# Layer A of a hybrid decoder step: value and gate units cut into eighths between the chunks of the recurrence

## The chip, the cores and the metric

The kernel runs on one core of one Trainium2 chip. A core has five engines that run at the same time, each through a list of instructions of its own in order: TensorE (PE in the profile; matrix products, with PEld for the loading of its stationary operand), VectorE (DVE), ScalarE (ACT), GpSimd (POOL) and SyncE (SP), which mostly issues transfers (DMA) between the large memory (HBM) and the core's own memory. Products land in banks of a small accumulator memory (PSUM), from which ACT or DVE copies them out ("evacuation"). The metric is the device time of one execution in microseconds.

## The reference, cut to what matters

One step of a two-layer decoder trunk for a prompt of 512 tokens and 8 sample sequences of 4 tokens (544 columns in all), width 1024, 16 heads of 64. Layer A is a recurrent mixer, layer B an attention layer. The change is in layer A alone:

```python
mixed = xn[None] + mu[:, None, None, :] * (prev - xn)[None]     # token shift, six mixtures
rkvz = jnp.einsum('pbtd,pde->pbte', mixed[:4], w_in)            # r, k, v, gate z: four 1024 x 1024 products
...
def wkv_step(state, inp):                                       # one token, every head; state is 64 x 64
    r, w, k, v, kk, b = inp
    sa = jnp.einsum('bhij,bhj->bhi', state, kk)
    state = state * w[:, :, None, :] - sa[..., None] * b[:, :, None, :] + v[..., None] * k[:, :, None, :]
    return state, jnp.einsum('bhij,bhj->bhi', state, r)
...
y = ((y - y_mean) * lax.rsqrt(y_var + GN_EPS)).reshape(B, T, D) * gn_w + gn_b
y = y + (jnp.sum(rh * kh * r_k, axis=-1, keepdims=True) * vh).reshape(B, T, D)
out = (y.astype(x.dtype) * jax.nn.silu(z)) @ w_out
return x + out, xn[:, -1], wkv, v
```

## The kernel before, in words

All activations lie feature by token: eight tiles of 128 features by 544 tokens. Each of the four input products and the output product is cut into eight units of 128 output features: units 0 to 7 are k, 8 to 15 r, 16 to 23 v, 24 to 31 the gate z, 32 to 39 the output. A unit is one call of `dense` (line 143): weights and activations are both split into a high and a low part, and three products (high x high, high x low, low x high) are summed, for eight slices of the inner dimension and two halves of the tokens (256 and 288 columns): 48 matmuls, all on line 152. For the units in `BOTH` the two halves go side by side in two banks; for the others one half follows the other. There are two such banks (`NPD`). `load_w` (line 126) fetches a unit's 512 KB, casts the high part on ACT (line 133) and subtracts for the low part on POOL (line 134).

The prompt's recurrence is done in chunks of 64 tokens, for eight pairs of heads (numbered p), eight chunks each. For a pair, `pre_a`, `pre_b` (with `gram`) and `pre_e` prepare decays, scaled keys and products within the chunks; `tinv` inverts the triangular parts of a group of two pairs (four groups) by 31 steps on DVE; `tmerge` and `prechain` join them. `feed(p, i)` makes what two chunks need of the values and keys (lines 624 to 644). `step(p, c2)` runs two chunks after one another: line 656 (first product) to PSUM, ACT's copy to `uv` (line 659), line 661 (second product), DVE's update of the state `mv` (line 671), and lines 675 and 678 (the output). Line 656 of the next chunk of the same pair needs line 671 of this one. `bonus(p)` prepares the term with the values, `gn` and `gn_apply` the norm per head, `sample_lanes` and `gn_sample` the sample tokens, `gate(p)` multiplies with the gate. After that the output product runs (from line 863), and layer B.

The order of the work is written out by hand in `PLAN` (line 60), one letter and number for a call: K k-units, H the hidden layers of decay and a, r r-units, v v-units, z gate units, X0 the splitting of v's input (`xvsplit`), X2 the mixing of z's input to a scratch (`zmix`), X1 its splitting (`xzsplit`), X3 that of r, a/b/e the preparation, T, M, P inverse and merges, F feeds, C steps, o bonus, h and S the samples, G, I, Y norms, g gates. A scheduler then orders the instructions of each engine by this order, by what depends on what and by an own estimate of times; an instruction that is ready may be put ahead of one that comes earlier in the plan. The eight split tiles of x (`NX`) are shared by k, r, v and z in turn, so v's split waits for the last r unit and z's for the last v unit. Value tiles have three buffers (`NV`), and `bonus` and held gate units share two (`NZ`, tag "Z").

In this plan the v units stand among the feeds and steps of the first pairs, and the gate units at the end and among the last steps. A gate unit that comes before its group's norm is held in a buffer until `gate` (lines 799 to 809).

## Time and profile before

| | |
|---|---|
| median of 3 runs | 1506.39 us (1498.46 to 1509.73) |
| the profiled execution | 1502.82 us, span from first to last instruction 1501.0 us |
| mean granted TensorE clock | 0.925 |
| busy over the span | PE 1373.4 (91%), PEld 1161.3, DVE 989.5, ACT 654.1, POOL 531.5 us |
| layer A, layer B | to about 664 us, and from there to the end |
| first and last chunk matmul (line 656) | 258.7 and 570.3 us |

All times within the profile count from the span's start. A line of a table gives for each engine the time in which it was executing something and the number of instructions; for TensorE the ends are modelled, so a busy TensorE may still be a slow one: the clock that its throttle granted stands beside it, as a share of full speed. In a timeline, lines start with the start and the duration in us; "idle before" names what the engine waited for.

### The profile page before, as it was taken

The numbers are of one execution on the slowest core, as the hardware profiler recorded it, in microseconds if no ns is written. First come the engines' busy times: TensorE is split into PE (matmuls) and PEld (weight loads), VectorE is DVE, ScalarE is ACT, GpSimd is POOL, SyncE is SP. The second block draws the span as 40 slices with busy tenths as digits, with TensorE's granted clock in tenths as the row PEclk, the third lists the DMA queues.
The fourth block names the chain that finished last, engine by engine and source line by source line (L and its number), as shares of the span: only waits on it lengthen the run. The fifth ranks groups of instructions, "written<-read, shape, count | busy, mean of one in ns | idle before, by whom it ended". The sixth has DMA issues, their size and how long they took to land.

```text
span 1501.0 us, 32052 instructions
## 1 busy us (share of the span) xinstructions
PE 1373.4 (91%) x12144; PEld 1161.3 (77%) x12144; DVE 989.5 (66%) x2612; ACT 654.1 (44%) x1808; POOL 531.5 (35%) x763
## 2 busy tenths in 40 slices
PE   2999879998988998999889899999999999999986
PEld 2777868676767666989777779989799888998776
DVE  7428594747677546798996869756568554685434
ACT  5448353333342355444543435545355543644321
POOL 6124365434545221796867686000000000000121
PEclk9999978765879698999999999999999999999988
DMA  4123636224243113456344583445734356344632
GB/s 145 46 80 132 201 97 157 62 56 122 66 123 72 38 43 116 150 165 202 90 136 147 171 269 120 145 142 164 256 111 151 129 194 232 103 152 136 227 116 102
DMA packets 140587, 201.26 MB, mean 134 GB/s; under 512 B 76864, under 2 KB 80640, under 8 KB 140432
## 3 DMA queue, kind: packets, MB, share of 16 engines
q1 hardware_dynamic: 121456, 137.48, 29.9%
q10 hardware_dynamic: 16416, 54.41, 10.8%
q0 software_dynamic: 2560, 7.31, 1.4%
q8 instruction: 96, 1.57, 0.4%
q14 instruction: 59, 0.48, 0.1%
HBM read 150.90 MB, written 34.87 MB: 124 GB/s over the span
## 4 chain that ended last, share of the span: by engine, by line
PE 42%; DVE 8%; DMA 3%; ACT 1%; issue 1%; SPq 1%; ACTq 0%; DVEq 0%
PE dps L152 29%; DVE wlo L139 4%; PE sps L1014 3%; PE ptp L1075 2%; PE spo L1170 2%; PE ops L1091 1%; DMA swp<-nat 1%; PE ops L1087 1%; PE sc L1126 1%; SPq L945 1%; PE sc L1137 1%; PE sc L1132 1%; PE vtp L975 1%; DVE swp L947 1%; DMA vc<-in_vc 1%
## 5 line engine op out<-in xcount | busy, mean ns | idle before, releaser
L152 PE MATMUL dps<-hn,whi 128*128 128x256 f32 (+1 forms) x2560 | 509.3, 294 | 8.2 <-DVE vt L964 2.4
L152 PEld LDWEIGHTS dps<-hn,whi 128*128 128x128 f32 x2560 | 405.3, 189 | 31.0 <-issue 19.0
L152 PE MATMUL dps<-hn,wlo 128*128 128x288 f32 (+1 forms) x1280 | 373.6, 292 | 5.0 <-DVE wlo L139 4.6
L138 ACT ACTIVATE whi<-wst,prm 128x128 fp32r<-128x128 f32 x640 | 202.1, 391 | 223.2 <-PE dps L152 173.4
L139 DVE SCALAR_TENSOR_TENSOR wlo<-wst,prm,whi 128x128 fp32r<-128x128 f32 x640 | 252.7, 450 | 35.2 <-ACT whi L138 34.6
L152 PE MATMUL dps<-x,whi 128*128 128x256 f32 (+1 forms) x1024 | 229.7, 317 | 27.4 <-ACT x L166 11.0
L152 PEld LDWEIGHTS dps<-hn,wlo 128*128 128x128 f32 x1280 | 242.8, 190 | 12.7 <-DVE wlo L139 7.6
L152 PEld LDWEIGHTS dps<-x,whi 128*128 128x128 f32 x1024 | 178.1, 207 | 52.1 <-issue 15.9
L134 POOL TENSOR_TENSOR wlo<-wst,whi 128x1024 fp32r<-128x1024 f32 x48 | 118.5, 2469 | 191.9 <-ACT whi L133 179.3
L152 PE MATMUL dps<-x,wlo 128*128 128x288 f32 (+1 forms) x512 | 158.2, 310 | 0.0
L152 PEld LDWEIGHTS dps<-x,wlo 128*128 128x128 f32 x512 | 106.4, 208 | 2.6 <-issue 1.8
L1100 POOL COPY qd<-Q 64x32 f32<-64x32 f32 x48 | 12.7, 265 | 266.4 <-DVE Q L950 143.2
L1298 POOL TENSOR_TENSOR sS<-sS,sT 128x256 f32<-128x256 f32 x128 | 102.6, 802 | 8.3 <-DMA sS<-in_stN 0.2
L152 PE MATMUL dps<-g,whi 128*128 128x288 f32 (+1 forms) x512 | 102.2, 296 | 2.9 <-DVE ho L869 1.4
L133 ACT CAST whi<-wst 128x1024 fp32r<-128x1024 f32 x48 | 50.3, 1047 | 93.8 <-PE dps L152 61.3
L152 PEld LDWEIGHTS dps<-g,whi 128*128 128x128 f32 x512 | 82.1, 191 | 6.4 <-DVE g L167 2.9
L946 DVE TENSOR_TENSOR nat<-nat,cosn 128x544 f32<-128x544 f32 x48 | 36.5, 760 | 66.4 <-DMA swp<-nat 65.5
L152 PE MATMUL dps<-g,wlo 128*128 128x256 f32 (+1 forms) x256 | 74.1, 290 | 0.0
L1029 ACT ACTIVATE s<-s,nm 128x256 f32<-128x256 f32 (+1 forms) x128 | 61.7, 484 | 20.1 <-DVE nm L1026 20.0
L1107 POOL COPY pk<-vt 128x32 f32<-128x32 f32 x24 | 5.4, 225 | 161.1 <-DVE vt L964 108.6
L1014 PE MATMUL sps<-K,Q 64*128 64x128 f32 (+1 forms) x384 | 55.1, 321 | 6.4 <-DVE st L1020 4.0
L307 DVE SCALAR_TENSOR_TENSOR mix<-xn,prm,mix 128x512 f32<-128x512 f32 x48 | 42.4, 884 | 26.0 <-ACT mix L305 25.9
(315 smaller groups left out, 2433.6 us busy)
## 6 DMA issues: line engine op xcount, KB each, us to landing
wst<-in_wb SPq DMA_DIRECT2D x88, 512.0 KB
kc<-in_kc ACTq DMA_DIRECT2D x48, 512.0 KB
vc<-in_vc ACTq DMA_DIRECT2D x48, 512.0 KB
wst<-in_wa SPq DMA_DIRECT2D x40, 512.0 KB
swp<-nat SPq DMA_DIRECT2D x192, 68.0 KB
out_kT<-K SPq DMA_DIRECT2D x24, 272.0 KB
out_vT<-vt SPq DMA_DIRECT2D x24, 272.0 KB
xt<-in_xT SPq DMA_DIRECT2D x8, 272.0 KB
```

What stands on the lines that cost most here:

```text
L133: nc.scalar.copy(hi, st)
L134: nc.gpsimd.tensor_tensor(lo, st, hi.bitcast(F32), op=ALU.subtract)
L138: nc.scalar.mul(hi[:, kt], st[:, kt], g)
L139: nc.vector.scalar_tensor_tensor(lo[:, kt], st[:, kt], g, hi[:, kt].bitcast(F32), op0=ALU.mult, op1=ALU.subtract)
L152: nc.tensor.matmul(ps[:, :n], lhsT=a[:, kt, :], rhs=x[:, c0:c0 + n], start=(kt == 0 and i == 0), stop=(kt == KT - 1 and i == 2))
L307: nc.vector.scalar_tensor_tensor(m[:, 0:NP_], xn[kt][:, 0:NP_], pv(s, kt), m[:, 0:NP_], op0=ALU.mult, op1=ALU.add)
L946: nc.vector.tensor_tensor(nat, nat, cosn, op=ALU.mult)
L1014: nc.tensor.matmul(ps[h][:, j, o], lhsT=Q[g][r, q], rhs=K[g][r, ks], start=True, stop=True)
L1029: nc.scalar.activation(s[:, b, lo:], s[:, b, lo:], AF.Exp, bias=nm[:, b:b + 1], accum_out=stats[:, b, h, 1:2])
L1075: nc.tensor.transpose(ps[:, b], st["s", l, h][:, b, half * P:(half + 1) * P], self.ident)
L1170: nc.tensor.matmul(po[32 * j:32 * j + 32, 0:256], lhsT=pT[:, i, 32 * j:32 * j + 32], rhs=vc[:, j], start=(i == 0), stop=False, skip_group_ ...
L1298: nc.gpsimd.tensor_tensor(s, s, t, op=ALU.add)
```

## The change

The dense units of v 2 to 7 and of z 0 to 7 are no longer calls of the plan. `dense` becomes a generator, `dense_pieces`, that yields ahead of each eighth of a unit (six matmuls). With `pin`, the first matmul of an eighth is tied behind the instruction that was written just before it on TensorE, so that the scheduler can't put it earlier. The plan's new call Q puts the 14 units (and between them the splitting of z's input) into a queue. `step` calls `pump` behind line 656 and behind the second product of each chunk: each call adds 0.875 to what is due, and eighths are written until that many are out, so 128 calls for 112 eighths. The call D writes what is left. The weights of a unit are loaded when the last eighth of the unit before is written.

A finished v unit and a held gate unit go to scratches in HBM (`scr["v"]`, `scr["z"]`); `values(p)` loads the values back at the first feed of a pair, `gate` loads its gate unit. Value tiles have four buffers. The plan is written anew: pairs 0 and 1 prepared and v 0 and 1 done first; then group by group, the steps of a group's two pairs taking turns, with the preparation of the next group's pairs between them; then the norms and gates of all.

```diff
-NV = 3
+NV = 4
+RATE = 0.875
-PLAN = """H0 K0 K1 H1 H2 H3 H4 H5 K2 H6 H7 K3 K4 K5 K6 K7 X3 r0 r7 N a0 r1 a1 b0 e0 b1 e1 T0
-X2 r2 r3 a3 r4 a2 r6 r5 X0 v1 v3 v0 b3 e3 M0 P0 F0 F1 F2 v2 C0 C1 b2 o1 F3 C2 C3 M1
...
-h0 h4 h5 h2 h6 h7 h1 S M6 P6 F24 F31 C30 z5 F25 C24 z0 Y0 G1 F26 I1 z2 z1 C19 C25 F27 G2 I2
-z3 C26 G0 C27 C31 G3 z4 g4 I0 g5 g3 g0 g1 g2 z6 I3 z7 g7 g6
+PLAN = """H0 K0 K1 H1 H2 H3 H4 H5 K2 H6 H7 K3 K4 K5 K6 K7 X3 r0 r1 N r2 a0 a1 r3 b0 b1 T0 r4 r5 e0 e1 r6 r7
+X0 X2 v0 v1 Q M0 P0 M1 P1
+F0 F1 a2 F4 F5 C0 F2 a3 C4 F6 b2 C1 F3 C5 b3 F7 T1 C2 C6 e2 C3 e3 o0 C7 o1
+M2 P2 M3 P3 F8 F9 a4 F12 F13 C8 F10 C12 F14 b4 C9 F11 a5 C13 F15 b5 T2 C10 C14 e4 C11 e5 o2 C15 o3
+M4 P4 M5 P5 F16 F17 a6 F20 F21 C16 F18 C20 F22 b6 C17 F19 a7 C21 F23 b7 T3 C18 C22 e6 C19 e7 o4 C23 o5
+M6 P6 M7 P7 F24 F25 o6 F28 F29 o7 G0 C24 F26 h0 h1 h2 h3 h4 h5 h6 h7 C28 F30 S I0 C25 F27 C29 F31 G1 C26 C30 I1
+C27 C31 D Y0 G2 I2 G3 I3 g0 g1 g2 g3 g4 g5 g6 g7
     def dense(self, w, xs, evac, both=False):
+        for _ in self.dense_pieces(w, xs, evac, both):
+            pass
+
+    def dense_pieces(self, w, xs, evac, both=False, pin=False):
...
+                m = nc.tensor.matmul(ps[:, :n], lhsT=a[:, kt, :], rhs=x[:, c0:c0 + n], start=(kt == 0 and i == 0),
+                                     stop=(kt == KT - 1 and i == 2))
+                if pin and i == 0:
+                    self.tc.keep_in_program_order(m)
         for hfs in (((0, 1),) if both else ((0,), (1,))):
-            ps = {hf: self.pd.tile([P, 512], F32, name="dps", tag="d") for hf in hfs}
+            ps = {}
             for kt in range(KT):
+                first = both or kt % 2 == 0
+                if first:
+                    yield
                 for hf in hfs:
-                    mm(ps[hf], hf, kt)
+                    if kt == 0:
+                        ps[hf] = self.pd.tile([P, 512], F32, name="dps", tag="d")
+                    mm(ps[hf], hf, kt, pin and first and hf == hfs[0])
...
+            queue, sent, due = [], [0], [0.0]
+
+            def advance():
+                while queue:
+                    if callable(queue[0]):
+                        queue.pop(0)()
+                        continue
+                    if next(queue[0], None) is not None:
+                        sent[0] += 1
+                        return
+                    queue.pop(0)
+
+            def pump():
+                due[0] += RATE
+                while queue and sent[0] < due[0]:
+                    advance()
...
             def feed(p, i):
                 bk, rh = BK[p], RH[p]
+                values(p)
...
                         nc.tensor.matmul(ps[r, o:o + 64], lhsT=WW[p][:, e, c2, h, :], rhs=mv[:, e, h, :],
                                          start=(e == 0), stop=True, skip_group_check=True)
+                    pump()
                     for h, r in ((0, RA), (1, RB)):
                         self.mv_("ue", uv[RA, e, h, :], ps[r, o:o + 64], h)
...
+                    pump()
                     if c < 7:
...
                 if hold:
-                    Z[p] = zp.tile([P, NT], F32, name="zg", tag="Z")
+                    Z[p] = True
+                    zt = zp.tile([P, NT], F32, name="zg", tag="Z")
...
-                self.dense(self.load_w(W[24 + p]), xz, evac, both=24 + p in BOTH)
+                for _ in self.dense_pieces(lambda: self.load_w(W[24 + p]), xz, evac, 24 + p in BOTH, True):
+                    yield True
+                if hold:
+                    nc.sync.dma_start(out=scr["z"][p], in_=zt)
...
+            def vlater(p):
+                t = vp.tile([P, NT], F32, name="vT", tag="V")
...
+                for _ in self.dense_pieces(lambda: self.load_w(W[16 + p]), xv, evac, 16 + p in BOTH, True):
+                    yield True
+                nc.sync.dma_start(out=scr["v"][p], in_=t)
+
+            def values(p):
+                if vT[p] is None:
+                    vT[p] = vp.tile([P, NT], F32, name="vT", tag="V")
+                    nc.sync.dma_start(out=vT[p], in_=scr["v"][p])
...
+                       Q=lambda p: queue.extend([vlater(i) for i in range(2, 8)] + [xzsplit]
+                                                + [zproj(i) for i in range(8)]))
```

## The prediction, made before the changed kernel was run

> **What bounds the kernel now.** I read the profile's page first (slices), then the busy time of the engines by stage, then the dense matmuls alone, then the timeline and the waits of TensorE.

> ```profile
> PEclk9999978765879698999999999999999999999988
> ```

> From the sixth to the sixteenth slice (37.5 us each, so about 190 to 600 us) TensorE's granted clock is mostly below full. The stretches of the kernel, cut at the first chunk matmul (258.70), at the end of the last chunk (574), at the first output projection (607.7) and at layer B (664), with their columns length, PE, PEld, DVE, ACT, POOL, clock, DMA share, GB/s:

> ```profile
> 125.00:200.00 75.00, 66.61 (x500) 58.38 (x499) 53.44 (x109) 39.22 (x84) 33.20 (x33) 0.95 0.55 171
> 200.00:232.00 32.00, 25.29 (x148) 20.42 (x149) 31.45 (x74) 16.68 (x35) 18.93 (x20) 0.57 0.28 84
> 232.00:258.70 26.70, 24.25 (x322) 21.80 (x321) 8.09 (x22) 8.79 (x19) 17.61 (x19) 0.94 0.70 166
> 258.70:574.00 315.30, 286.11 (x3478) 214.19 (x3480) 198.66 (x599) 123.43 (x344) 125.46 (x214) 0.77 0.28 76
> 574.00:607.70 33.70, 30.75 (x203) 26.47 (x200) 23.20 (x38) 17.26 (x27) 9.02 (x7) 0.91 0.38 117
> 607.70:664.00 56.30, 52.15 (x390) 49.25 (x389) 45.87 (x57) 22.79 (x43) 48.98 (x47) 1.00 0.51 167
> 664.00:1501.00 837.00, 793.75 (x6575) 700.24 (x6574) 564.72 (x1600) 360.77 (x1139) 232.77 (x357) 0.98 0.49 159
> ```

> The recurrence takes 315.30 us at a mean clock of 0.77. TensorE is idle for only 29 us of it; its 286 us of work are 286.11 x 0.77 = 220 us at full clock. So 66 us go to the low clock and 29 to idling. The next views say when the clock is low. First the dense matmuls alone (tile dps; PE, clock, DMA share, GB/s) in 10 us steps:

> ```profile
> 300.00:310.00 10.00, 0.00 (x0) 0.50 0.29 68
> 310.00:320.00 10.00, 0.02 (x1) 0.50 0.14 40
> 320.00:330.00 10.00, 8.58 (x48) 0.80 0.28 69
> 330.00:340.00 10.00, 0.00 (x0) 1.00 0.42 91
> ```

> The clock is half while only small matmuls run, and returns when a whole dense unit (48 matmuls) comes by. Then, from the timeline, what half clock costs, in pairs of cold and warm rows:

> ```profile
> 301.64 0.48 PE L675 MATMUL cps<-rT,mv 64*64 64x64 f32 x4
> 302.05 0.48 PE L678 MATMUL cps<-Q,uv 128*64 128x64 f32 x4
> ...
> 542.69 0.33 PE L675 MATMUL cps<-rT,mv 64*64 64x64 f32 x4
> 542.95 0.34 PE L678 MATMUL cps<-Q,uv 128*64 128x64 f32 x4
> ```

> ```profile
> 320.79 0.63 PE L152 MATMUL dps<-x,whi 128*128 128x256 f32 x2
> ...
> 321.43 0.63 PE L152 MATMUL dps<-x,whi 128*128 128x256 f32 x2
> ```

> ```profile
> 577.89 0.51 PE L152 MATMUL dps<-x,whi 128*128 128x256 f32 x2
> ...
> 584.09 1.03 PE L779 MATMUL ssg<-sqg,sel 128*2 128x512 f32 x4
> ```

> A chunk's group of four starts 0.41 us after the one before when cold, 0.26 when warm; three dense matmuls take 0.64 us cold. A whole unit takes 584.09 - 577.89 = 6.2 us warm, so 0.78 us for an eighth. Of waits, TensorE has few in the recurrence:

> ```profile
> PE cps L675 <- DVE mv L671: 8.4, 8, 2.3
> PE atp L524 <- DVE ak L517: 4.7, 1, 4.7
> ```

> So the bound of this stage is TensorE at a low clock; the chain of a chunk comes second.

> **The change, part by part.** Everything before 125 us and after 664 us stays. I go by stages.

> (1) Up to the first chunk. Now it starts at 258.70. The new order has only pairs 0 and 1 prepared and units v0, v1 done by then; one unit (v3, 6.2 us) and the preparation of pairs 2 and 3 go behind the start, merges of pair 1 come ahead of it. The mix of the gate input (X2) comes later, behind X0, on ACT and VectorE, but only the eighths of z need it. In 200:232 VectorE is busy 31.45 of 32 us while TensorE has 25.29 us at clock 0.57; this is where the preparation of pairs 2 and 3 stands in the way of the split of x for v. With it gone I take 20 us off: 6 of v3 and 14 of the 32. At worst only the 6 go, at best 32 (all of that stretch's length). Start at 239 (227 to 253).

> (2) Work in the recurrence. Dense matmuls now:

> ```profile
> 258.70:574.00 315.30, 66.37 (x384) 59.39 (x384) 2.62 (x6) 6.42 (x18) 0.77 0.28 76
> ```

> 384 are 8 units. The queue holds 14 (six v, eight z), 112 eighths for 128 pumps at 0.875, so all go between chunks: 6 x 6.2 = 37 us more. Of the pairs' own work, two pre_a, gram and pre_e come in and two merges' share, the last group norm and the sample norm go out:

> ```profile
> L411 PE MATMUL lps<-hid,lb 64*128 64x288 f32 (+1 forms) x36 | 17.3, 624 | 1.8 <-ACT tw L413 1.8
> ...
> L607 PE MATMUL wwp<-TT,ak 64*64 64x64 f32 x512 | 16.2, 248 | 0.1
> ```

> Eight of L411's make a pre_a (3.8 us), L607 costs 2.0 us a pair; with their neighbours I take +13 and -10, net 3 (bounds -10 and 13). Work at full clock: 220 + 37 + 3 = 260 us.

> (3) What comes on top of it. Now it is 66 for the clock and 29 for idling, 95 on 220. An eighth stands behind the first and behind the second matmuls of a chunk (1.75 of them per chunk, 64 chunks), so while ACT copies and VectorE updates the state TensorE streams 0.78 us of dense work. In 315 us that is an eighth each 2.8 us; the stretches of 20 us without any dense matmul go. I take the clock's loss as 28 (66 less more than half). Idling: each pin holds what is queued behind it on TensorE: the next chunk's small matmuls, and who waits for them, ACT's copy of uv and VectorE's state update. A pinned eighth waits for its weights (cast on ACT, subtraction on POOL), for a free bank of two, that is for the last evacuation, and, at the ninth unit, for xz. I take 32 for idling (29 now), as the fill takes about as much as the new holds give. 260 + 28 + 32 = 320. Bounds: 260 + 10 + 15 = 285 and, if the loss stays at the present ratio, 260 x 315 / 220 = 372. So C31 ends at 239 + 320 = 559, where it is 574 now.

> (4) Other engines and queues in it. VectorE has 198.66 us now; pre_a and pre_b of two pairs and the evacuations of five gate units bring it to some 225 of 320, no bound. POOL subtracts the weights' parts of six more units there,

> ```profile
> L134 POOL TENSOR_TENSOR wlo<-wst,whi 128x1024 fp32r<-128x1024 f32 x48 | 118.5, 2469 | 191.9 <-ACT whi L133 179.3
> ```

> 6 x 2.47 = 15 us more on 125. What waits in POOL's line behind one of them for 2.5 us is the copy of a chunk's values (uv), and so L661; that is part of the 32 for idling. SyncE gets 28 DMA issues more (6 + 8 stores, 6 + 8 loads of 272 KB each). The DMA share is 0.28 here, and their issue is as bsum's now:

> ```profile
> L687 SPq DMA_DIRECT2D bsum<-scr_b x8: 319/382/526, 183.4 to 423.5; - x8
> L689 POOL TENSOR_TENSOR bsum<-bsum,vT x8: 1327/1336/2468, 233.2 to 451.1; 128x544 f32<-128x544 f32 x8
> ```

> 28 x 0.38 = 11 us on a queue of 320 us: hidden by loads that are issued early (the first bsum 50 us before its use). If the cover goes, an issue stands behind a wait of SyncE, whose largest sum is

> ```profile
> SPq L129 <- POOL wlo L134: 37.1, 4, 22.5
> ```

> and a feed waits for vT. I cost it at 0, at most one such 22.5.

> (5) From the last chunk to the output projection, now 33.7 us of which TensorE works 30.75, nearly all gate units. These are gone; what is left is the chain of the last norm:

> ```profile
> 575.15 2.71 PE L772 MATMUL cps<-Y,cblk 128*128 128x512 f32 x4
> ...
> 584.09 1.03 PE L779 MATMUL ssg<-sqg,sel 128*2 128x512 f32 x4
> ```

> ```profile
> 587.43 0.95 SPq L783 DMA_DIRECT2D rows<-rs  x2
> ```

> L779 needs L772's squares, ready at about 578.6, and stood 5.5 us behind a dense unit. So 33.7 - 5.5 = 28; reloads of z (two buffers) may add 6, so 28 to 36; I take 29. The projection then starts after some 20 us of idle TensorE, so one or two us cold: 58 for its 56.3.

> Sum: 239 + 320 + 29 + 58 = 646 for layer A where it is 664, so 18 us less, and the profiled execution (1502.82, span 1501.0) would take 1485. It lies 3.57 below the median of 1506.39, so I say 1488.

> [...] The clock falls here in a stretch that isn't idle (PE, clock, DMA share, GB/s in 2 us steps):

> ```profile
> 394.00:396.00 2.00, 1.70 (x26) 1.00 0.93 333
> 396.00:398.00 2.00, 1.30 (x20) 1.00 0.04 15
> 398.00:400.00 2.00, 1.33 (x21) 0.77 0.03 8
> ```

> TensorE was busy for two thirds of the time and lost the clock. [...]

> **The rivals.** (a) The clock holds throughout: loss 0 to 5, idling 32. The recurrence is 260 + 3 + 32 = 295, the whole 25 less than above: 1463. For it: at 330:340 the clock stays at 1.00 with no dense matmul at all, so little is needed to hold it. Against: the rows at 394.
> (b) No gain: the pins hold as much as the clock gives. The recurrence at 335 to 340, the whole 1503 to 1508. For it: the chains of the inverse stay on VectorE inside the groups, and L675 already waits for VectorE (8.4 us), atp too (4.7 at once).
> (c) Slower: once cold it stays cold. In the old order whole units brought the clock back (8.58 us of dense in 320:330); in the new one no dense run is longer than 0.78 us warm, so a window is a mixture. If the clock is half for three quarters of the recurrence, work goes at 0.26/0.41 = 0.63 of the pace there, 260 / (0.25 + 0.75 x 0.63) = 360, with 30 of idling 390: 70 more than above, 1558. It decides from 340 on, that is a loss of 80 on 260; at half the recurrence cold it is 260 / 0.815 + 30 = 349, 1517. A second way to the same place: z and bonus share two buffers (tag Z), and reloads issued far ahead, as bsum's, can keep both from the evacuation of a unit, which keeps a bank, which keeps a pin.

> **How the numbers follow.** Anything within 15 us (1%) of 1506 can't be told from no change. Forecast as summed (1470 to 1491) 0.35, (a) with all below 1470 0.17, (b) (1491 to 1521) 0.26, (c) above 1521 0.22. So faster 0.52, same 0.26, slower 0.22. The likeliest case's own range is 1470 to 1491. The range for 8 in 10 leaves out the far end of (a), below 1450 (0.08), and of (c), above 1535 (0.12).

> **What would show it.** Clock in the recurrence above 0.9 and its length near 320 (step 3); first L656 near 239 (step 1); 14 units' matmuls between first and last chunk (step 2); L779 right behind L772 at the end, no dense unit between (step 5). Wrong would be: a clock of 0.7 or below with eighths spread evenly (c); long rows of dense matmuls waiting for an evacuation, weights or xz, with L656 and L661 queued behind (b); a recurrence that starts no earlier than 255.

## The result, and the profile after

The changed kernel takes 1574.07 us (median of 4 runs, 1571.99 to 1576.79) and the kernel before 1507.7 in the same series (1498.46 to 1509.73). The ratio is 1.0454, with a 95% interval of 1.0406 to 1.0502: slower by 4.5%, where 1488 us had been forecast. The profiled execution has a span of 1575.0 us, 74.0 more than before.

The slices of the changed kernel's page, 39.4 us each (tenths busy, tenths of full clock):

```profile
PE   2999869989879798368988999999999999999986
...
PEclk9998966978669779669999999999999999999988
```

The low clock from the sixth to the sixteenth slice, which was to go, is still there, and two slices follow (630 to 710 us) with TensorE at 3 and 6 tenths. The stages, cut as the prediction cut them (length, PE, PEld, DVE, ACT, POOL, clock, DMA share, GB/s):

```profile
120.00:200.00 80.00, 70.91 (x522) 62.57 (x522) 59.44 (x118) 37.61 (x77) 33.23 (x34) 0.90 0.45 138
200.00:252.20 52.20, 39.47 (x485) 32.31 (x484) 40.47 (x71) 30.12 (x65) 28.95 (x39) 0.60 0.48 135
252.20:628.50 376.30, 334.11 (x3643) 256.93 (x3641) 214.74 (x620) 125.27 (x345) 138.91 (x224) 0.80 0.32 88
628.50:690.00 61.50, 22.88 (x75) 13.14 (x76) 28.29 (x46) 17.42 (x34) 20.09 (x24) 0.61 0.34 103
690.00:738.20 48.20, 44.15 (x336) 43.34 (x336) 32.98 (x44) 17.80 (x36) 44.48 (x45) 0.97 0.51 169
738.20:1575.00 836.80, 796.87 (x6576) 701.57 (x6574) 558.81 (x1600) 360.49 (x1139) 217.07 (x336) 0.98 0.48 158
```

The recurrence takes 376.3 us where it took 315.3. TensorE's clock is 0.80 after 0.77, so it hardly rose. From the last chunk to layer B it is 109.7 us where it was 90.0. The start is 6.5 us earlier, and layer B is as it was.

For comparing runs the recurrence is measured below from the start of the first chunk's first product (line 656 before, 693 after) to that of the last chunk's (some 4 us less than above), and "the end" from there to layer B's first matmul. These are the rows of before and after, all instructions and then the dense matmuls alone. First, before:

```profile
258.70:570.40 311.70, 282.82 (x3450) 212.27 (x3452) 196.74 (x592) 120.28 (x337) 125.46 (x214) 0.77 0.28 74
```

```profile
258.70:570.40 311.70, 66.37 (x384) 59.39 (x384) 0.77 0.28 74
```

Then after:

```profile
252.20:624.40 372.20, 330.91 (x3618) 254.50 (x3616) 213.25 (x615) 124.43 (x341) 138.91 (x224) 0.79 0.32 87
```

```profile
252.20:624.40 372.20, 132.46 (x660) 105.27 (x660) 0.79 0.32 87
```

The 60.5 us come apart from these rows. The dense matmuls take 132.46 us instead of 66.37 (+66.1), all other matmuls 330.91 - 132.46 = 198.5 instead of 216.4 (-18.0), and TensorE idles for 41.3 instead of 28.9 (+12.4). A dense matmul in the recurrence takes 132.46 / 660 = 201 ns, where it took 173. That the small matmuls got faster isn't shown: by the counts of the rows they are 108 fewer (2958 for 3066), and a dense matmul is counted here to its modelled end, which overlaps the small one behind it. Counted from each start to the next, a small one takes 70.8 ns where it took 71.5. Nor did the time at the low clock shrink: by the records of the granted clock, it is 154 us of these 372.2 (TensorE busy for 135 of them), and was 144 us (busy for 134).

With the start (-6.5), the recurrence (+60.5), the end (113.5 instead of 93.2, +20.3) and layer B (-0.3) this is the whole of the 74.0.

### The profile page after: what moved, and what is told of

Same layout as the page of the kernel before. It is cut to its first block, busy times and chain, and to the rows that moved or that the text cites. A ratio compares the mean times of both kernels' runs of the same rounds, so it can differ in the third digit from the quotient of the medians.

```text
span 1575.0 us, 32083 instructions
## 1 busy us (share of the span) xinstructions
PE 1399.3 (89%) x12144; PEld 1177.9 (75%) x12144; DVE 994.8 (63%) x2608; ACT 649.7 (41%) x1804; POOL 527.0 (33%) x763
## 4 chain that ended last, share of the span: by engine, by line
PE 40%; DVE 8%; DMA 2%; ACT 1%; issue 1%; SPq 0%; ACTq 0%; DVEq 0%
PE dps L158 28%; DVE wlo L140 3%; PE sps L1077 3%; PE ptp L1138 2%; PE spo L1233 2%; PE ops L1154 1%; PE ops L1150 1%; PE sc L1189 1%; DVE swp L1010 1%; DMA kc<-in_kc 1%; DMA swp<-nat 1%; DMA vc<-in_vc 1%; PE vtp L1038 1%; PE sc L1195 1%; PE sc L1200 1%
## 5 line engine op out<-in xcount | busy, mean ns | idle before, releaser
L158 PE MATMUL dps<-x,whi 128*128 128x256 f32 (+1 forms) x1024 | 248.7, 332 | 26.3 <-ACT x L179 15.1
L140 DVE SCALAR_TENSOR_TENSOR wlo<-wst,prm,whi 128x128 fp32r<-128x128 f32 x640 | 244.0, 437 | 34.6 <-ACT whi L139 34.2
L158 PE MATMUL dps<-g,whi 128*128 128x288 f32 (+1 forms) x512 | 107.3, 306 | 22.9 <-ACT g L179 14.6
L158 PEld LDWEIGHTS dps<-g,whi 128*128 128x128 f32 x512 | 85.8, 200 | 28.6 <-ACT g L179 16.9
L134 ACT CAST whi<-wst 128x1024 fp32r<-128x1024 f32 x48 | 50.2, 1045 | 86.2 <-PE dps L158 58.5
```

The costliest lines, as they stand in the source:

```text
L134: nc.scalar.copy(hi, st)
L140: nc.vector.scalar_tensor_tensor(lo[:, kt], st[:, kt], g, hi[:, kt].bitcast(F32), op0=ALU.mult, op1=ALU.subtract)
L158: m = nc.tensor.matmul(ps[:, :n], lhsT=a[:, kt, :], rhs=x[:, c0:c0 + n], start=(kt == 0 and i == 0), stop=(kt == KT - 1 and i == 2))
```

## The experiments

The table has for each run: the dense matmuls between first and last chunk, their time and ns of each; TensorE's other busy time and its idle time there; the mean granted clock; the recurrence; the end; the median. Except for the medians, the values are from window rows like those above. Times in us. Layer B, whose code no run changes, takes 834 to 850 us in these profiled executions, so a difference of some 15 us between two whole times need not be the edit's.

| run | dense | their time | ns each | other | idle | clock | recurrence | end | median |
|---|---|---|---|---|---|---|---|---|---|
| before | 384 | 66.4 | 173 | 216.4 | 28.9 | 0.77 | 311.7 | 93.2 | 1507.7 |
| after | 660 | 132.5 | 201 | 198.5 | 41.3 | 0.79 | 372.2 | 113.5 | 1574.1 |
| e1_nopin | 569 | 94.2 | 165 | 211.2 | 26.3 | 0.79 | 331.7 | 123.3 | 1555.4 |
| e2_whole | 571 | 94.5 | 165 | 217.0 | 30.3 | 0.77 | 341.8 | 121.9 | 1564.9 |
| e3_oldorder | 624 | 127.1 | 204 | 210.3 | 19.3 | 0.77 | 356.6 | 92.7 | 1546.8 |
| e5_early | 660 | 131.0 | 199 | 198.9 | 48.7 | 0.79 | 378.6 | 118.4 | 1596.3 |
| e8_oldhalf | 378 | 84.0 | 222 | 223.3 | 24.2 | 0.72 | 331.5 | 101.9 | 1529.9 |
| e9_oldhalf_nopin | 416 | 70.0 | 168 | 216.3 | 35.5 | 0.76 | 321.8 | 92.7 | 1527.6 |
| e10_rate | 423 | 87.7 | 207 | 212.9 | 51.4 | 0.75 | 351.9 | 131.9 | 1579.3 |
| e6_tail | 648 | 129.2 | 199 | 206.8 | 43.4 | 0.79 | 379.4 | 91.9 | 1566.3 |
| e4_apart | 0 | 0 | | 266.8 | 58.6 | 0.57 | 325.3 | 167.6 | 1626.8 |
| e11_burst | 660 | 130.9 | 198 | 196.9 | 46.3 | 0.79 | 374.1 | 117.3 | 1579.7 |
| e12_wholepin | 618 | 107.6 | 174 | 205.3 | 51.4 | 0.78 | 364.2 | 117.1 | 1572.4 |
| e13_nopin_tail | 545 | 90.0 | 165 | 222.8 | 31.7 | 0.78 | 344.4 | 95.3 | 1543.2 |
| e14_cover | 283 | 49.7 | 176 | 261.2 | 49.9 | 0.65 | 360.8 | 103.0 | 1558.7 |
| e15_ctrl | 478 | 80.5 | 168 | 219.8 | 26.2 | 0.77 | 326.5 | 88.3 | 1520.5 |
| e16_allz | 576 | 94.8 | 165 | 224.1 | 22.6 | 0.76 | 341.4 | 90.9 | 1529.7 |
| e17_four1 | 186 | 31.7 | 171 | 241.7 | 63.9 | 0.66 | 337.4 | 130.7 | 1590.8 |
| e18_four8 | 0 | 0 | | 258.0 | 59.6 | 0.60 | 317.6 | 168.9 | 1617.4 |
| e19_four8 | 186 | 47.2 | 254 | 236.4 | 64.7 | 0.64 | 348.3 | 134.6 | 1601.3 |

The clock column follows the amount of dense work between the chunks more than the way it is cut: 0.57 and 0.60 with none, 0.64 to 0.66 with 186 to 283 matmuls, 0.72 to 0.77 with 378 to 478, and 0.76 to 0.79 with 545 to 660.

### Order, pins, eighths

The first theory was that the order costs the time. At the change of groups the next group's inverse, merges and first feeds stand alone. TensorE's timeline at the second such place of the changed kernel:

```profile
423.81 0.90 PE L612 MATMUL tps<-ident,TT 32*32 32x32 f32 x25 [1.39 <-DMA TT<-tt]
...
428.71 2.88 PE L643 MATMUL wwp<-TT,ak 64*64 64x64 f32 x64
439.94 2.46 PE L546 MATMUL gps<-bk,rowb 64*64 64x128 f32 x26 [8.34 <-DVE bk L497]
...
448.23 2.75 PE L643 MATMUL wwp<-TT,ak 64*64 64x64 f32 x64
...
455.23 0.48 PE L693 MATMUL cps<-mv,ak 128*64 128x64 f32 x2 [2.48 <-DVE mv L105]
```

The second pair's merge (448) stands behind a later pair's products (439.94), for which TensorE waited 8.34 us, and the next chunk comes at 455. Four runs set this against the pins and the eighths.

e1_nopin takes the pins away:

```diff
-                if pin and i == 0:
+                if False:
```

> The changed kernel with its eighths not pinned; order and queue as they are. Order theory (the loss lies at the three group boundaries, some 72 us, and in the tail, 61.5 us for 33.7; pins and eighths cost nothing): within 1% of the changed kernel's 1574, the boundaries stay. Pin theory (pinned eighths hold up the chunks' small matmuls): below 1530, the four groups at some 78 us each get shorter. If the pins are what keeps the clock up, slower than 1590 with a lower clock inside the groups.

Measured: 1555.38, ratio 1.0329 (1.0276 to 1.0382), between the theories' values. The recurrence is 40.5 us shorter, its dense matmuls take 165 ns each, and the end is 9.8 longer. So the order theory fell as the only cause, and the pins do cost: e1 is 18.7 us faster than the changed kernel. The 40.5 us are more than that price, as without pins the scheduler puts work elsewhere. Ahead of the first chunk stand 968 dense matmuls instead of 864, about two units more, and the first chunk comes only 3.4 us later; layer B took 848.6 us in this execution for 837.1.

e2_whole also writes a unit at once:

```diff
-                while queue and sent[0] < due[0]:
-                    advance()
+                while queue and sent[0] + 8 <= due[0]:
+                    n = sent[0] + 8
+                    while queue and sent[0] < n:
+                        advance()
```

> The changed kernel's order, its 14 units written whole (one each time that eight eighths are due) and not pinned. Order theory: 1560 to 1610, since boundaries and tail are those of the changed kernel and the groups can only lose. Eighths-and-pins theory: 1520 or below, near the kernel before, since whole units are what that had.

Measured: 1564.92, ratio 1.0384 (1.0330 to 1.0439), as the order theory has it. Without pins, eighths or whole units make no difference to a dense matmul (165 ns both): the scheduler puts the eighths together itself. Of e1's dense matmuls 65% stand in unbroken rows of twelve or more on TensorE, of the changed kernel's 27%.

e3_oldorder keeps pins and eighths, in the order of before (two of the lines that differ from before's plan):

```diff
-X2 r2 r3 a3 r4 a2 r6 r5 X0 v1 v3 v0 b3 e3 M0 P0 F0 F1 F2 v2 C0 C1 b2 o1 F3 C2 C3 M1
+X2 r2 r3 a3 r4 a2 r6 r5 X0 v1 v3 v0 Q b3 e3 M0 P0 F0 F1 F2 C0 C1 b2 o1 F3 C2 C3 M1
...
-z3 C26 G0 C27 C31 G3 z4 g4 I0 g5 g3 g0 g1 g2 z6 I3 z7 g7 g6
+C26 G0 C27 C31 D G3 g4 I0 g5 g3 g0 g1 g2 I3 g7 g6
```

> The order of the kernel before for preparation, feeds, steps, norms and gates; only v 2, 4, 5, 6, 7 and the eight gate units go through the queue as pinned eighths. Order theory: 1470 to 1520, at or below the kernel before, since its preparation of a group lies beside another group's chunks. Eighths-and-pins theory: 1550 or more, as the changed kernel.

Measured: 1546.84, ratio 1.0259 (1.0191 to 1.0327), again between. The old order gives back the whole loss of the end (92.7), and the idling is the lowest of all runs (19.3). But the dense matmuls are as slow as in the changed kernel (204 ns).

e5_early moves the next group's preparation, inverse and merges ahead:

```diff
-F0 F1 a2 F4 F5 C0 F2 a3 C4 F6 b2 C1 F3 C5 b3 F7 T1 C2 C6 e2 C3 e3 o0 C7 o1
-M2 P2 M3 P3 F8 F9 a4 F12 F13 C8 F10 C12 F14 b4 C9 F11 a5 C13 F15 b5 T2 C10 C14 e4 C11 e5 o2 C15 o3
+F0 F1 a2 F4 F5 C0 b2 F2 C4 a3 F6 C1 b3 T1 F3 C5 e2 F7 C2 M2 P2 e3 C6 M3 P3 C3 o0 F8 F9 C7 o1 F12 F13
+a4 C8 b4 F10 C12 a5 F14 C9 b5 T2 F11 C13 e4 F15 C10 M4 P4 e5 C14 M5 P5 C11 o2 F16 F17 C15 o3 F20 F21
...
```

> The changed kernel with the next group's preparation, inverse, merges and first feeds moved ahead in the plan, beside the chunks of the group before; eighths, pins and the rest of the tail unchanged. Order theory: the three boundaries (72 us in all) shrink to below 35 us together, 1520 to 1540. Eighths-and-pins theory: 1565 to 1585, nothing gained. If the inverse is late whatever the place (its 31 steps on VectorE), a gain of less than 15.

Measured: 1596.32, ratio 1.0604 (1.0557 to 1.0650), slower than the changed kernel. The waits of TensorE between first and last chunk begin with

```profile
PE wps L606 <- DMA TT<-tt: 13.8, 3, 10.3
```

The merge in the same place still waits for the inverse, up to 10.3 us at once. Another place in the plan didn't make it earlier, so what would fill the group changes stays open.

### What a pinned eighth costs, and what lies at the end

e8_oldhalf leaves five gate units for the end, in the old order (its plan line against e3's; it also reorders the queue's v units and moves two bonus calls):

```diff
-RATE = 0.875
+RATE = 0.5
...
-C26 G0 C27 C31 D G3 g4 I0 g5 g3 g0 g1 g2 I3 g7 g6
+C26 G0 C27 C31 G3 I0 I3 D g4 g5 g3 g0 g1 g2 g7 g6
```

> The order of the kernel before with pinned eighths, written at half a call's rate, so that about five gate units are left and come behind the last norm's matmuls instead of between the chunks. Cover theory (five gate units used to lie free of cost under the chain of the last norms; between the chunks they cost their time, and the end is no shorter without them): the recurrence falls from 357 us (first run in the old order) to 305 to 325, the stretch from the last chunk to layer B stays 93 to 98, in all 1495 to 1520. Pin theory (the holds are what costs): 1535 or more, the recurrence above 340. If both ends gain, below 1490.

> As the run in the old order with half the rate, the eighths not pinned. Pin theory: 15 to 40 us below the pinned one, as the changed kernel lost 40 in its recurrence when its pins went. Cover theory alone: the same as the pinned one within 1%.

Measured: 1529.88 with pins, ratio 1.0175 (1.0103 to 1.0246), and 1527.55 without (e9), 1.0147 (1.0078 to 1.0216). Neither theory had this. Five units fewer shortened e3's recurrence by 25.1 us, but with as many dense matmuls as before (378 and 384) it is 20 us longer than before. 17.6 of these are the dense matmuls themselves (222 ns for 173). Without pins they are fast again (168 ns). As in e1, work went ahead of the first chunk: 78 dense matmuls more than in e8. e9 gains 9.7 us in the recurrence and 9.2 at the end by it, but its first chunk comes 8.3 later, and layer B takes 850.1 us for 834.3 with the same instructions. That spread stays unexplained.

e10_rate does the same in the new order (rate 0.55, `C27 C31 Y0 G2 I2 G3 I3 D`), e6_tail moves the samples' and the third group's norm:

```diff
-                    y = sp.tile([32, P], F32, name="yt", tag="yt", bufs=1)
+                    y = sp.tile([32, P], F32, name="yt", tag="yt", bufs=5)
...
-M6 P6 M7 P7 F24 F25 o6 F28 F29 o7 G0 C24 F26 h0 h1 h2 h3 h4 h5 h6 h7 C28 F30 S I0 C25 F27 C29 F31 G1 C26 C30 I1
-C27 C31 D Y0 G2 I2 G3 I3 g0 g1 g2 g3 g4 g5 g6 g7
+M6 P6 M7 P7 F24 F25 o6 F28 F29 o7 G0 C24 h0 h1 h2 h3 h4 h5 h6 h7 F26 S I0 C28 G1 F30 C25 F27 I1 C29 F31 G2 C26 Y0 C30 I2
+C27 C31 D G3 I3 g0 g1 g2 g3 g4 g5 g6 g7
```

> The changed kernel's order and pins with a rate of 0.55: five gate units left, which come behind the last norms' matmuls. Cover theory: the recurrence falls from 372 to 325 to 345, the stretch from the last chunk to layer B stays at 110 to 120, in all 1525 to 1550. Order theory alone (boundaries and the samples' place in the end): 1560 to 1580, since both are as before.

> The changed kernel with the samples' norm (its eight loads, five buffers instead of one) and the third group's norm written before the last chunks. If the samples' place makes the end long: the stretch from the last chunk to layer B falls from 113 to 90 to 98, in all 1550 to 1562. If the end is the last norms' chain in any case: 1568 to 1580.

Measured: e10 1579.31 (ratio 1.0496, 1.0432 to 1.0560): no gain, the cover theory missed. The recurrence is 20 shorter and the end 18 longer. e6 1566.25 (1.0407, 1.0334 to 1.0480), with the end as expected and the whole 4 us above its range. The changed kernel's largest waits of TensorE at the end were

```profile
PE ysp L787 <- DMA yt<-sys: 16.6, 7, 4.5
PE dps L158 <- ACT g L179: 14.6, 3, 7.9
```

and in e6

```profile
PE dps L158 <- ACT g L179: 14.8, 6, 6.6
...
PE ysp L787 <- DMA yt<-sys: 0.2, 1, 0.2
```

The 16.6 us for the samples' eight loads through one buffer are gone, and the end is 21.6 shorter, by both moves together. But 7.2 came back in the recurrence, and the whole can't be told from the changed kernel by its interval.

### The clock

These kernels have pins and eighths in common where dense matmuls are slow. Is it the clock? Two neighbouring stretches of the changed kernel, all instructions:

```profile
555.00:573.60 18.60, 18.60 (x116) 14.10 (x114) 5.25 (x18) 4.26 (x11) 5.21 (x9) 0.50 0.07 21
573.60:597.50 23.90, 21.75 (x236) 15.56 (x235) 14.21 (x38) 10.23 (x24) 12.48 (x17) 1.00 0.43 113
```

and their dense matmuls:

```profile
555.00:573.60 18.60, 9.48 (x30) 7.40 (x30) 0.50 0.07 21
573.60:597.50 23.90, 10.67 (x62) 8.12 (x61) 1.00 0.43 113
```

TensorE is busy all through the first one, half of it with dense matmuls, and stays at half clock to its end. In the second, less busy and with nearly the same share, the clock stays full. So in these two stretches the mixture that a pinned eighth per few small matmuls makes kept a full clock for 23.90 us, but brought a lost one back only behind 18.60. The theory from here on: only a stretch filled mostly with dense matmuls brings it back. Three runs tested it first.

e4_apart writes the v units ahead of the first merge and the gate units behind the last chunk (rate 0):

```diff
-X0 X2 v0 v1 Q M0 P0 M1 P1
+X0 X2 v0 v1 Q0 D M0 P0 M1 P1
...
-C27 C31 D Y0 G2 I2 G3 I3 g0 g1 g2 g3 g4 g5 g6 g7
+C27 C31 Q1 D Y0 G2 I2 G3 I3 g0 g1 g2 g3 g4 g5 g6 g7
```

> The changed kernel's order with no dense unit between the chunks: the six v units are written ahead of the first merge, the eight gate units behind the last chunk. Clock theory (once the clock has fallen only a window of some 3.4 us filled mostly with dense matmuls brings it back; small matmuls alone never do, however busy TensorE is): the granted clock falls soon after the recurrence starts and stays at half, 0.6 or less as a mean from first to last chunk, and the recurrence takes 290 to 320 us. If the clock comes back by itself when TensorE is busy: 0.75 or more, and a recurrence of 240 to 270. In all 1580 to 1620 for the dense work that stands alone.

Measured: 1626.82, ratio 1.0807 (1.0718 to 1.0895). The recurrence is 325.3 (5 above the range) at a clock of

```profile
281.50:606.80 325.30, 266.75 (x2946) 184.88 (x2944) 182.31 (x579) 94.51 (x291) 99.10 (x201) 0.57 0.25 61
...
480.00:505.00 25.00, 25.00 (x196) 17.81 (x192) 11.00 (x38) 5.90 (x22) 6.82 (x12) 0.50 0.33 75
```

The second row shows 25 us in which TensorE is busy without a break and stays at half clock; all but eight of its 196 matmuls have at most 128 columns. But the clock did come back four times without a dense matmul, once at 395 us:

```profile
391.80:395.20 3.40, 3.40 (x13) 2.08 (x12) 0.67 (x3) 0.61 (x2) 0.00 (x0) 0.50 0.51 93
396.00:400.00 4.00, 4.00 (x61) 3.16 (x57) 2.60 (x12) 1.32 (x6) 1.39 (x4) 1.00 0.62 144
```

What TensorE did in the first of these rows was mostly this:

```profile
L510 PE MATMUL bps<-tw,bones 128*128 128x256 f32 x2 | 1.2, 715 | 0.0
L510 PE MATMUL bps<-tw,bones 128*128 128x288 f32 x2 | 1.2, 687 | 0.0
```

In the 3.4 us ahead of each of the four returns (one step of the clock in these traces, see the last section), matmuls of 128 rows and 256 to 512 columns took 58 to 90% of the time. So the dense ones weren't needed: what the four returns of this trace share is wide matmuls ahead of them.

e11_burst (rate 0.5, and `B2`, two pinned units at a time, ahead of `M2`, `M4` and `M6`) and e12_wholepin (e2's edit with the pins kept):

> The changed kernel with its rate at 0.5 and, at each of the three group boundaries, two pinned units in one piece. Clock theory: each piece fills a boundary's idle time and brings the clock back, so the recurrence falls from 372 to 335 to 355 us, in all 1535 to 1560. If the boundaries only get longer by the pieces (12.6 us each at full clock): 1570 to 1600.

> The changed kernel with its units pinned but written whole, eight eighths each time that eight are due. Clock theory: a whole unit is longer than a window and brings the clock back, so the loss by the clock falls below 50 us (59 with eighths) and the recurrence to 335 to 355, in all 1540 to 1560. Pin theory (any pin holds the chunks up, and a long piece more): 1575 to 1620.

Measured: e11 1579.74 (1.0489, 1.0421 to 1.0556): the clock theory missed here, the mean clock is the changed kernel's (0.79), and the group changes just got longer (28, 45 and 41 us without a chunk's first product; 18, 36 and 27 in the changed kernel). e12 1572.40 (1.0446, 1.0381 to 1.0510), neither: whole units make the pinned dense matmuls fast (174 ns), but TensorE idles for 51.4 us, 10 more, and the recurrence gains only 8. The clock theory missed here too: busy time and mean clock give a loss of 69 us (312.84 at 0.78), as in the changed kernel by the same sum (330.91 at 0.79), and not one below 50.

So the clock alone doesn't make the dense matmuls slow: 165, 174 and 201 ns stand in e1, e12 and the changed kernel at the same mean clock. The records of the granted clock split them further:

| run | start at half clock | ns at half clock | ns at full clock |
|---|---|---|---|
| before | 99 of 384 | 236 | 154 |
| after | 160 of 660 | 287 | 175 |
| e1_nopin | 63 of 568 | 266 | 155 |
| e12_wholepin | 125 of 618 | 279 | 149 |
| e17_four1 | 42 of 186 | 260 | 148 |
| e19_four8 | 104 of 186 | 306 | 191 |

Against before, the changed kernel has the same share at half clock (24% for 26%), and each dense matmul is dearer at either clock. So the 28 ns more are the price of short pieces. Against e1, some half of the 36 ns is the larger share at half clock. As ends are modelled and a short row of matmuls ends more often, part of the pieces' price may be the way busy time is counted; how much isn't shown. The pins cost through dearer pieces where these are short (201 ns a matmul in the changed kernel, 174 in e12), and through waits where they are long (51.4 us of idling in e12, 41.3 in the changed kernel).

e13_nopin_tail has e1's and e6's edits together:

> The changed kernel with both gains so far: its eighths not pinned, and the samples' norm and the third group's norm written earlier. If the two add up: 1525 to 1545. If the end is the last norms' chain whatever stands before it: 1550 to 1560.

Measured: 1543.18, ratio 1.0247 (1.0186 to 1.0308), as expected if the two add up: half of the loss is back. Its rows (recurrence, end) are

```profile
254.80:599.20 344.40, 312.75 (x3517) 233.14 (x3516) 214.43 (x618) 121.82 (x346) 137.98 (x225) 0.78 0.34 92
599.20:694.50 95.30, 68.73 (x434) 59.06 (x430) 67.73 (x90) 35.74 (x62) 67.73 (x71) 0.82 0.50 154
```

What is left against before is +32.7 in the recurrence (23.6 of it dense matmuls), -3.9 at the start, +2.1 at the end, +2.7 in layer B, together the 33.6 of its span of 1534.6.

### Gate units at the end

Before, the end held 620 matmuls in 93.2 us; e13's holds 434 in 95.3. So some four gate units lay in before's end and lengthened nothing. e14_cover leaves five for it in e13 (rate 0.55, `D` behind `I3`). e15_ctrl has before's plan in the changed code, with units whole and not pinned. e16_allz then moves only the gate units, ahead of the last steps:

```diff
-F17 C16 o3 F18 C17 T3 F19 C18 C11 M7 P7 F28 X1 F29 o7 F30 C28 C29 F20 o6 F21 C20 F22 C21 h3 F23 C22 C23
+F17 C16 o3 F18 C17 T3 F19 C18 C11 M7 P7 F28 X1 F29 o7 F30 C28 C29 z0 F20 o6 F21 C20 z1 F22 C21 z2 h3 F23 C22 z3 C23 z4
...
-z3 C26 G0 C27 C31 G3 z4 g4 I0 g5 g3 g0 g1 g2 z6 I3 z7 g7 g6
+C26 G0 C27 C31 G3 g4 I0 g5 g3 g0 g1 g2 I3 g7 g6
```

> The run without pins and with the early samples' norm, and the rate at 0.55, so that five gate units come behind the last norms' matmuls. Cover theory (those units cost nothing there and 28 to 32 us between the chunks): the recurrence falls from 344 to 305 to 325 us, the end stays at 92 to 102, in all 1500 to 1525. If they cost as much at the end as between the chunks: 1535 to 1550.

> The plan of the kernel before in the code of the changed one: v units whole and kept, gate units whole and not pinned, held ones stored to the scratch and loaded back. If the scratches and the rest of the code cost nothing: within 1% of the kernel before. If the trips of the gate units cost: 1520 or more.

> As the control, with one thing moved: all eight gate units, whole and not pinned, stand among the steps before the last ones, none is left for the end. Cover theory: the recurrence gets 25 to 35 us longer than the control's and the end not more than 8 shorter, in all 20 to 30 above the control. If more dense work between the chunks pays for itself in clock: within 8 of the control or below it.

Measured: e14 1558.65 (1.0377, 1.0310 to 1.0443), slower than e13 and above both expectations: with 283 dense matmuls between the chunks instead of 545 the mean clock is 0.65, where it was 0.78.

```profile
254.90:615.70 360.80, 310.89 (x3253) 221.48 (x3252) 208.13 (x605) 113.45 (x328) 124.51 (x215) 0.65 0.29 78
```

e15 1520.45 (1.0116, 1.0057 to 1.0175), e16 1529.72 (1.0174, 1.0104 to 1.0243). e15's recurrence and end, then e16's:

```profile
260.10:586.60 326.50, 300.29 (x3552) 226.66 (x3554) 206.47 (x608) 128.46 (x348) 130.15 (x217) 0.77 0.29 79
586.60:674.90 88.30, 72.65 (x518) 66.68 (x515) 56.13 (x83) 35.06 (x63) 55.73 (x50) 0.92 0.49 153
```

```profile
260.10:601.50 341.40, 318.85 (x3641) 242.27 (x3643) 195.38 (x605) 123.35 (x345) 136.14 (x223) 0.76 0.30 81
601.50:692.40 90.90, 62.92 (x428) 53.68 (x426) 69.05 (x82) 31.56 (x60) 69.03 (x74) 0.84 0.51 154
```

The control already differs from before: two units (94 matmuls) went from the end into the recurrence, probably since a stored gate unit no longer keeps its buffer. It got 14.8 us longer and the end 4.9 shorter. e16 moved two more (98): 14.9 longer, and the end 2.6 longer, not shorter. Together four units cost 29.7 us between the chunks and gave 2.3 at the end; the two of e16, with nothing else changed, are the cleaner half of it. e16 lies 9.3 above its control (16.4 by the spans), less than the 20 to 30 expected, as the control had already moved two of the four; against before it is 1.7%. e15's 1.2% is just past its limit of 1%, but the trips to the scratch by themselves can't be told from this shift, nor from layer B's 844.1 us for 837.4, and stay open.

### Four units whole, or in 32 pieces

e17_four1 is e4 with one whole pinned gate unit in the middle of each group; the rest comes at the end:

```diff
-F0 F1 a2 F4 F5 C0 F2 a3 C4 F6 b2 C1 F3 C5 b3 F7 T1 C2 C6 e2 C3 e3 o0 C7 o1
+F0 F1 a2 F4 F5 C0 F2 a3 C4 F6 b2 C1 F3 C5 b3 B1 F7 T1 C2 C6 e2 C3 e3 o0 C7 o1
...
```

> As the run with no dense unit between the chunks (297 of 325 us at half clock), with one whole pinned gate unit in the middle of each of the four groups and four at the end. Clock theory (a window filled with dense matmuls brings the clock back, a busy TensorE then keeps it): the clock rises behind each of the four units and stays up until the next stall, so less than 240 us at half clock, and the recurrence takes 315 to 335 us though it has four units (24 us at full clock) more to do. In all 1585 to 1615.

> The same four gate units between the chunks, as pinned eighths spread evenly over them at a rate of 0.25. Clock theory: no window is filled mostly with dense matmuls, the clock doesn't come back, 280 us or more at half clock, the eighths run at half speed (some 45 us), and the recurrence takes 345 to 375 us. If only the amount of dense work counts and not how it is spread: the same as the run with the whole units within 8 us.

> In the run before this one no eighth was written between the chunks, since the count of those sent started with the v units; here it starts at zero, so the four gate units do come as 32 pinned eighths, one in four calls. Clock theory: 270 us or more at half clock (229 with the four units whole), the eighths for the most part at half speed, and the recurrence takes 342 to 375 us (337 with whole units). If only the amount of dense work counts: at half clock within 20 us of the whole units' 229, the recurrence at 330 to 342.

Measured: e17 1590.81, ratio 1.0519 (1.0458 to 1.0580), in its range, with a recurrence 2.4 us above its range. e18 told nothing about eighths, as it had no dense work between its chunks; it repeats e4 (clock 0.60, recurrence 317.6 for 325.3, which is also the spread to be reckoned with). e19 1601.25, 1.0641 (1.0403 to 1.0878); of its two runs, 1589.9 and 1612.6, the profile shows the second. The dense matmuls of e17,

```profile
280.60:618.00 337.40, 31.72 (x186) 28.30 (x186) 0.66 0.27 70
```

and of e19:

```profile
282.50:630.80 348.30, 47.24 (x186) 36.30 (x186) 0.64 0.27 69
```

The same 186 matmuls take 171 ns each in four pieces and 254 ns in 32, and the recurrence is 10.9 us longer. Beside those 15.5 us little differs. By the split above, about half of them come from more matmuls at half clock (104 for 42), and the other half from a dearer matmul at either clock. By the records of the granted clock e19 is at half clock for 253 us, e17 for 228, e4 for 281 (the 297 of e17's expectation is too much: at a mean of 0.57, 325.3 us hold 280) and its repeat e18 for 256. So e19 lies below the 270 that the clock theory expected, but it can't be told from e18, which has no dense matmul at all, and whether four whole units really brought back some 25 us of clock stays open, as e4 and e18 lie as far apart. The recurrences lie 8 us apart between e4 and e18, so of the 10.9 only the part in the dense matmuls is certain.

## Why the prediction was wrong, step by step

By the prediction's own arithmetic the recurrence of the changed kernel is 334.11 x 0.80 = 267 us of work at full clock, 67 lost to the clock and 42 of idling. It had taken 260, 28 and 32.

- Step (2), the work at full clock: right within 7 us. All 14 units came between first and last chunk (672 matmuls). The sum was partly luck: at full clock a unit takes 48 x 175 ns = 8.4 us in pieces, where the prediction took 6.2, while the small matmuls, for which it added 3 us, came 108 fewer.
- Step (3), the clock's loss: **the step that failed**. "I take the clock's loss as 28"; it stayed at 67, as it was (66). The prediction reasoned that "the stretches of 20 us without any dense matmul go", and took their going for a full clock. They did go inside the groups (none is longer than 8 us there), but the half clock didn't go with them: it is 154 us for 144, some 57 of them at the three group changes and 97 inside the groups. Spreading the dense work didn't raise the mean here: e1 has two stretches of 78 and 69 us with next to no dense matmul, at clocks of 0.62 and 0.70, and still the same mean as the changed kernel (0.79). And the pinned eighths among small matmuls left a lost clock at half for 18.60 us, though TensorE was busy for all of them (9.48 of them dense, clock 0.50). Each dense matmul also got dearer: in the table every kernel with pinned eighths has 198 to 254 ns for one, and every other one 165 to 176. The clock is lost again at the group changes, here the second and the third:

```profile
425.00:460.00 35.00, 23.56 (x372) 18.51 (x366) 17.88 (x39) 15.84 (x34) 14.84 (x24) 0.55 0.38 107
...
530.00:552.00 22.00, 15.80 (x350) 13.57 (x350) 1.05 (x4) 6.75 (x17) 11.78 (x12) 0.50 0.42 118
```

- Step (3), idling: 42 for 32. The group changes and pins account for it: without pins 26.3 in the same order, with the old order 19.3.
- Step (5), the end: 109.7 us for 29 + 58, namely 61.5 up to the output projection and 48.2 from there. It had counted the last norm's chain, but not what the new plan puts ahead of it: eight loads of the samples through one buffer (16.6 us of waiting; the end 21.6 shorter when they and the third group's norm were moved). That the gate units' going would give only 5 us here was right: four of them cost 29.7 between the chunks and gave back 2.3. The one or two us cold in the 58 were an estimate; the stretch from 690 us began at a clock of 0.55 for 3.40 us and had 0.97 as a whole.
- Step (1), the start: 252.2 for 239, inside its bounds of 227 to 253. VectorE's load was not the only bound; TensorE's first two waits from 185 to 252 us are others:

```profile
PE wwp L643 <- ACT TT L105: 7.8, 1, 7.8
PE dps L158 <- ACT x L179: 6.4, 2, 5.5
```

- Step (4), other engines and queues at 0: nothing contradicts it. TensorE's largest waits between first and last chunk are

```profile
PE cps L714 <- DVE mv L710: 9.4, 6, 3.0
PE gps L546 <- DVE bk L497: 8.3, 1, 8.3
PE cps L693 <- DVE mv L105: 5.0, 2, 2.5
```

  and none is for a reloaded value.

The misses add up: 13 at the start, 56 in the recurrence (39 clock, 7 work, 10 idling), 23 at the end, together the 92 by which layer A ended late (738 for 646). Rival (c) had the side, and its "a window is a mixture" fits the row of 18.60 us (9.48 of them dense). Its "once cold it stays cold" doesn't: the clock was half for 154 of 372.2 us, not for half or three quarters of the recurrence, and its sign, "a clock of 0.7 or below", didn't come (0.80). 36 of the 92 us came from the start and the end, which (c) doesn't speak of, so much of its nearness is luck.

## What to carry to other kernels

Don't count on filler work to raise TensorE's clock because it leaves no stretch without it. Here the mean clock went with the amount of dense work (0.57 and 0.60 with none between the chunks, 0.76 to 0.79 with 545 to 660 matmuls), and none of the ways to cut, pin or order the same 14 units took it above 0.79. Short pieces were dearer than whole ones (254 ns a matmul in e19, 171 in e17), and pins keep the scheduler from putting work into free time elsewhere. An eighth at half clock took 6 x 287 ns = 1.7 us in the changed kernel, half of a step of 3.41 us, and behind the half-clock steps with wide matmuls for less than 60% the clock came back in 35 of 911 (table below). Whether whole units placed where the clock has just been lost would pay isn't shown: e11's didn't. Before moving work off the end of a stage, see whether it lies there under a chain that is as long without it: then it is nearly free where it is, and costs its time elsewhere (29.7 us for four units here).

## What the runs showed of the hardware

| clock in a step | what the step held | the next step at full clock |
|---|---|---|
| half | dense matmuls for 60% or more | 88 of 102 |
| half | wide matmuls for 60% or more | 122 of 147 |
| half | wide matmuls for less | 35 of 911 |
| half | no wide matmul | 7 of 630 |
| full | TensorE busy for 80% or more | 759 of 774 |
| full | busy for less than 60% | 2 of 86 |

At half clock 811 steps had TensorE busy for 80% or more, and the clock was full behind 157 of them. Of these 157 the step held wide matmuls for 60% or more in 122. Of the 69 full steps that were busy for 80% or more without a wide matmul, 62 kept the clock; of the 630 half ones without a wide matmul, 7 were followed by a full one. What in a matmul makes the difference isn't shown; their busy times are modelled. The stretches of full and of half clock in the changed kernel are multiples of that step: 3.4, 6.8, 13.7, 17.1, 20.5 and 23.9 us occur.
